# Eleven pairs of projections as block products in a stage of their own

## The chip, the cores and the metric

The kernel runs on one core of a Trainium2 chip. The metric is the device time of one execution in microseconds (us). Three runs of the kernel before took 1333.49, 1348.46 and 1333.42 us; their median is 1333.49 us.

## The reference

One encoder layer over 512 tokens of width 1024: a SwiGLU feed-forward layer, LayerNorm, a token mixer of three branches, LayerNorm, a second feed-forward layer, LayerNorm. All data are float32.

```python
proj = u @ w_in      # latents | dilated q, k, v | memory q | 3 gates
y_a = mla_attention(c_q, c_kv, k_rope, ...) @ w_br_mla       # 8 heads
y_b = dilated_attention(dil_cols) @ w_br_dil                 # 3 groups x 4 heads of 128
y_c = memory_attention(memq_cols, mem, w_mem_kv) @ w_br_mem  # 4 heads of 128
merged = sigmoid(g0) * y_a + sigmoid(g1) * y_b + sigmoid(g2) * y_c
h = layer_norm(ALPHA * h + merged @ w_o)
```

The change concerns the columns of `u @ w_in` that give dilated queries and keys (24 slices of 128 columns), memory queries (4 slices) and the gates (3 x 8 slices).

## The kernel before, in words

**Numbers.** Each float32 operand is kept as a high part `h` and a rest `l`. A weight tile is loaded from DRAM into one of three slots `raw` (SyncE, SP, issues it, L84), ScalarE (ACT) copies it to the high part (L87) and VectorE (DVE) subtracts that from it for the rest (L88). A product is three matmuls, high x high, high x rest, rest x high (`mm3`, L98 to L100). A result is split in the same way (L92, L93).

**Projections.** `proj` loads one 128-column slice of a weight (0.5 MB) and multiplies it with `u` in 8 steps of 128 rows: 24 matmuls that each stream 512 columns. `gate` puts a tanh behind it. `Gates.fill(n)` issues n of a gate's 8 steps, as work for TensorE (PE) between other steps. `y_a`, `y_b` and `y_c` multiply a branch's output with `w_br`: 12 matmuls of 512 columns each, two of them from one loaded weight.

**Quads.** The two feed-forward layers compute a pair of projections (gate and up) together: the pair is cut into blocks, and 7 block products of 12 matmuls with 256 columns, with sums of blocks on either side, give both results (`quad_load`, `quad_conv`, `quads`). I call one such pair a quad; it has 84 matmuls. Its sums of weights are formed by accumulating transfers that GpSimd (POOL) issues (L246, L247) onto parts that SP loaded (L243 to L245).

**Stages** (us of the span). Feed-forward layer 1 up to 345, with its quads from 33 to 229; memory keys and values, LayerNorm up to 402; latent attention up to 516; then `dil_v(0)`, six `y_a`, six projections `dil_proj` for head 0 and two `y_a` up to 604; four dilated heads up to 791; memory attention, with `y_b` and gates between its steps, up to 905; `y_c` and `w_o` up to 965; LayerNorm and layer 2 with its quads (1022 to 1205) to the end.

**A dilated head** is `dil_scores`, then cover work on PE, `dil_mix`, `dil_tr`, more cover work, `dil_pv`. Between scores and mix the row maxima and sums change their layout through DRAM: ACT stores them (L790, L791), POOL's queue loads them back (L792, L793), DVE combines them (L799 to L809) and scales the probabilities (L813). `dil_tr` transposes them (L825), ACT and DVE split them, and `dil_pv` uses them. In heads 0 to 2 the cover is four projections of the next head ahead of the mix and two behind the transposes; in head 3 it is gates.

**Order.** PE and SP run what is written in the order in which it is written (a manual schedule); the other engines' order is a scheduler's, except in the quads, where it is written too. Weight loads may be issued up to 200 priorities ahead, but SP's queue is in order: a load that waits for a free `raw` slot holds back all that are behind it.

Of the kernel before, what the change touches and what calls it, by code (L numbers as in the profile page):

```python
# [33 lines left out]
def build(tc, a, out):  # L34
# [141 lines left out]
    class FFN:  # L176
# [46 lines left out]
        def sums(self, xr):  # L223
# [10 lines left out]
            xh, xl = self.xT  # L234
            for i, j, c in ((1, 0, 0), (2, 1, 0), (4, 1, 1)):
                self.X[i] = tuple(x[:, 4 * j:4 * j + 4, c * 256:(c + 1) * 256] for x in self.xT)

        def quad_load(self, f):
            src = self.wgu[f]
# [40 lines left out]
        def quads(self, f0, f1, r):  # L280
            V = nc.vector
            m, u, sg = self.m, self.u, self.sg
            with tc.manual_schedule(engines={mybir.EngineType.DVE, mybir.EngineType.Activation, mybir.EngineType.Pool}):
# [5 lines left out]
                for f in range(f0, f1 + 1):  # L289
                    if f + 2 < f1:  # L290
                        r[f + 2] = self.quad_load(f + 2)
                    if f == f1 - 1:
                        self.s_r.close()
                        self.hc = pool("hc" + self.n, stack=self.stack, side="right")
# [11 lines left out]
                    if f == f1 - 1:  # L306
                        self.early = {c: self.h_pair(c, 0, S) for c in range(2)}
                    if prev is not None:
                        p, pa, pW = prev
                        self.prod(pa, pW, 4)  # L310
                        nc.scalar.activation(sg[:, 256:], pa, AF.Silu)
                        V.tensor_tensor(out=self.h(p), in0=u, in1=sg, op=OP.mult)
                    if f == f1:
                        break
                    self.prod(a, W, 6)
# [12 lines left out]
                    nc.scalar.activation(sg[:, :256], sg[:, :256], AF.Silu)  # L328
# [14 lines left out]
        def down(self, hf, toks, done, order=range(NF // 2), have={}, dest={}, mid=None):  # L343
# [17 lines left out]
            return kept  # L361

# [335 lines left out]
    mla_pv(7)  # L698
    s_a.close()


    s_b = ExitStack()
    bp = pool("dil", stack=s_b)
# [29 lines left out]
    def dil_proj(g, h, j):  # L733
        ps = proj(a["wdqk"][h, g, j], f"dp{g}{h}{j}")
        hl = bp.tile([P, 2, S], F32R, name=f"dhl{g}{h}{j}", tag="dqk", bufs=7)
        hi, lo = hl[:, 0], hl[:, 1]
        if g == 0:
            split(hi, lo, ps)
        else:
            split(hi.rearrange("p (r j) -> p r j", r=4), lo.rearrange("p (r j) -> p r j", r=4), ps.rearrange("p (j r) -> p r j", r=4))  # L740
        qkB[g, h, j] = (hi, lo, hl)

# [112 lines left out]
    def y_a(f):  # L855
        ps = branch_y(0, f, oA)
        nc.vector.scalar_tensor_tensor(out=acc[f], in0=acc[f], scalar=1.0, in1=ps, op0=OP.add, op1=OP.mult)
# [9 lines left out]
    s_oa.close()  # L867
# [16 lines left out]
    gb = Gates(1, [])  # L884
    for h in range(4):
        dil_scores(h)
        if h < 3:
            for g in range(2):
                for j in range(2):
                    dil_proj(g, h + 1, j)  # L890
        else:
            for f in range(4):
                sgB[f] = obp.tile([P, S], F32, name=f"sgB{f}", tag="sgB", bufs=4)
                gb.todo.append((1, f, sgB[f]))
            gb.fill(23)
        dil_mix(h)
        dil_tr(h)
        if h < 3:
            dil_proj(2, h + 1, 0)
            dil_proj(2, h + 1, 1)  # L900
        else:
            gb.fill(9)
        dil_pv(h)
        if h == 1:
            dil_v(1)
    s_q.close()
# [10 lines left out]
    qC, pC, tC, sgC = {}, {}, {}, {}  # L917

    def mem_q(h):
        ps = proj(a["wmq"][h], f"mq{h}")  # L920
        q = (cp.tile([P, S], F32R, name=f"mqh{h}", tag="mqh", bufs=2), cp.tile([P, S], F32R, name=f"mql{h}", tag="mql", bufs=2))
        split(q[0], q[1], ps)
        qC[h] = q
# [30 lines left out]
    def gate_c(f):  # L954
        sgC[f] = ocp.tile([P, S], F32, name=f"sgC{f}", tag="sgC", bufs=6)
        gate(2, f, sgC[f])
# [6 lines left out]

    mem_q(0)
# [3 lines left out]
    y_b(1)  # L968
    gate_b(4)
    mem_scores(0)  # L970
    y_b(2)
    gate_b(5)
    y_b(3)
    mem_tr(0)
    mem_q(1)
    mem_pv(0)
    gate_b(6)
    mem_scores(1)
    y_b(4)
# [76 lines left out]
    s_w.close()  # L1056
    s_acc.close()
# [54 lines left out]
def _pack(inputs):  # L1112
# [44 lines left out]
    A["wdqk"] = np.stack([np.stack([np.stack([fm(dil[:, j, g, h])[0] for j in range(2)]) for g in range(3)]) for h in range(4)])  # L1157
# [3 lines left out]
    A["wmq"] = fm(w_in[:, C_MQ:C_G])  # L1161
# [38 lines left out]
```

## Time and profile before

| | |
|---|---|
| median of three runs | 1333.49 us |
| profiled execution | 1332.55 us, span 1330.8 us |
| granted TensorE clock, mean | 0.997 |
| PE busy | 1310.9 us, 99% of the span |
| DVE, ACT, POOL busy | 65%, 46%, 8% |
| instructions of the span | 20,324 |

PE is the busy engine in every stage, so a stretch of the span is as long as PE's work in it, and time is lost where PE waits. The page gives busy shares, the chain that ended last, the costliest groups of instructions and the DMA issues; the stages are seen in a table of windows, single steps in the timeline of an engine.

### The profile page before, as it was taken

How to read it: one execution, taken by the hardware profiler on the slowest of the kernel's cores; microseconds unless marked ns; L12 is line 12 of the kernel's file. 1: busy time of each engine (PE TensorE's matmuls, PEld its weight loads, DVE VectorE, ACT ScalarE, POOL GpSimd, SP SyncE). 2: the span in 40 equal slices, each digit the busy share in tenths (PEclk: the TensorE clock that was granted, in tenths of full speed). 3: DMA queues.
4: the chain of work that ended last, by engine and by line, in shares of the span. 5: the costliest groups of instructions: out<-in, count | busy, mean ns of one | idle time of the engine just before them, and what ended most of it. 6: DMA issues, size and time to landing. Idle time of an engine off the chain costs nothing.

```text
span 1330.8 us, 20324 instructions
## 1 busy us (share of the span) xinstructions
PE 1310.9 (99%) x8036; PEld 1176.8 (88%) x8036; DVE 862.4 (65%) x1359; ACT 609.0 (46%) x987; POOL 109.0 (8%) x140
## 2 busy tenths in 40 slices
PE   8999999999999999999999999999999999999997
PEld 7999999888878879988899888888889999998885
DVE  8777776454748994435554556545798777774547
ACT  6555554433346773324334343343335555553332
POOL 1111110000101001000000000000011211100001
PEclk9999999999999999999999999999999999999998
DMA  8877775342544224322323323223666877764241
GB/s 259 211 185 203 190 199 176 118 143 95 163 154 143 58 64 79 127 95 88 72 80 103 96 65 127 80 80 95 215 220 188 207 183 199 193 184 131 99 155 64
DMA packets 70736, 185.75 MB, mean 140 GB/s; under 512 B 15728, under 2 KB 16368, under 8 KB 70640
## 3 DMA queue, kind: packets, MB, share of 16 engines
q1 hardware_dynamic: 49680, 159.73, 35.8%
q0 software_dynamic: 16736, 24.68, 11.4%
q8 instruction: 63, 1.03, 0.3%
q10 hardware_dynamic: 4224, 0.03, 0.2%
q14 instruction: 33, 0.27, 0.1%
HBM read 173.90 MB, written 7.37 MB: 136 GB/s over the span
## 4 chain that ended last, share of the span: by engine, by line
PE 91%; DVE 4%; DMA 2%; ACT 2%; issue 1%; POOL 0%; SPq 0%; POOLq 0%; DVEq 0%; ACTq 0%
PE dn L100 6%; PE dn L98 6%; PE dn L99 6%; PE ga L98 5%; PE ga L100 5%; PE ga L99 5%; PE dp L98 3%; PE dp L99 3%; PE dp L100 3%; PE g L98 3%; PE g L99 3%; PE gc L100 3%; PE gc L98 3%; PE g L100 3%; PE gc L99 3%; PE v L98 2%
## 5 line engine op out<-in xcount | busy, mean ns | idle before, releaser
L88 DVE TENSOR_TENSOR w<-raw,w 128x1024 fp32r<-128x1024 f32 x159 | 193.7, 1221 | 133.5 <-ACT w L87 129.0
L87 ACT ACTIVATE w<-raw 128x1024 fp32r<-128x1024 f32 x159 | 167.7, 1055 | 214.3 <-PE dp L99 45.9
L100 PE MATMUL dn<-w,hcl 128*128 128x512 f32 x320 | 124.6, 389 | 0.1
L99 PE MATMUL dn<-w,hch 128*128 128x512 f32 x320 | 124.5, 389 | 0.0
L98 PE MATMUL dn<-w,hch 128*128 128x512 f32 x320 | 124.5, 389 | 0.0
L263 DVE TENSOR_TENSOR w<-raw,w 128x1024 fp32r<-128x1024 f32 x78 | 95.1, 1219 | 1.9 <-ACT w L260 1.7
L260 ACT ACTIVATE w<-raw 128x1024 fp32r<-128x1024 f32 x78 | 82.0, 1052 | 8.8 <-DMA raw<-in_wgu 8.8
L98 PE MATMUL g<-uh,w 128*128 128x512 f32 x192 | 75.2, 391 | 0.0
L98 PE MATMUL dp<-uh,w 128*128 128x512 f32 x192 | 75.2, 391 | 0.0
L100 PE MATMUL g<-uh,w 128*128 128x512 f32 x192 | 74.8, 389 | 0.0
L100 PE MATMUL dp<-uh,w 128*128 128x512 f32 x192 | 74.8, 389 | 0.0
L99 PE MATMUL dp<-ul,w 128*128 128x512 f32 x192 | 74.7, 389 | 0.0
L99 PE MATMUL g<-ul,w 128*128 128x512 f32 x192 | 74.7, 389 | 0.0
L100 PEld LDWEIGHTS dn<-w,hcl 128*128 128x128 f32 x320 | 60.1, 188 | 13.1 <-DVE hcl L93 0.5
L99 PEld LDWEIGHTS dn<-w,hch 128*128 128x128 f32 x320 | 60.1, 188 | 12.5
L98 PEld LDWEIGHTS dn<-w,hch 128*128 128x128 f32 x320 | 60.1, 188 | 12.2
L93 DVE TENSOR_TENSOR hcl<-ha,hch 128x1024 fp32r<-128x1024 f32 (+2 forms) x35 | 35.1, 1009 | 53.3 <-ACT hch L92 53.3
L92 ACT ACTIVATE hch<-ha 128x1024 fp32r<-128x1024 f32 (+2 forms) x35 | 30.8, 887 | 74.9 <-PE dn L99 72.8
L263 DVE TENSOR_TENSOR w2l<-raw,w2h 128x1024 fp32r<-128x1024 f32 x39 | 47.8, 1225 | 20.6 <-ACT w2h L260 20.5
L328 ACT ACTIVATE sg<-sg 128x256 f32<-128x256 f32 x39 | 16.3, 419 | 86.2 <-DVE sg L327 86.2
L247 POOL DMA_DIRECT2D raw<-in_wgu x39 | 33.6, 862 | 248.8 <-DMA raw<-in_wgu 235.9
L93 DVE TENSOR_TENSOR hcl<-hb,hch 128x1024 fp32r<-128x1024 f32 (+2 forms) x20 | 20.2, 1011 | 49.7 <-ACT hch L92 49.7
(890 smaller groups left out, 4052.4 us busy)
## 6 DMA issues: line engine op xcount, KB each, us to landing
raw<-in_wgu SPq DMA_DIRECT2D x86, 512.0 KB, 5.8
raw<-in_wd SPq DMA_DIRECT2D x47, 512.0 KB, 3.4
raw<-in_wgu POOLq DMA_DIRECT2D x78, 256.0 KB, 5.7
raw<-in_wg SPq DMA_DIRECT2D x24, 512.0 KB, 3.6
raw<-in_wdqk SPq DMA_DIRECT2D x24, 512.0 KB, 3.3
raw<-in_wgu SPq DMA_DIRECT2D x42, 256.0 KB, 5.4
raw<-in_wo SPq DMA_DIRECT2D x16, 512.0 KB, 4.3
raw<-in_wv SPq DMA_DIRECT2D x12, 512.0 KB, 3.3
```

Of the source, the lines that this page charges most:

```text
L87: nc.scalar.activation(hi[:, c], raw[:, c], AF.Copy)
L88: (eng or nc.vector).tensor_tensor(out=lo[:, c], in0=raw[:, c], in1=hi[:, c].bitcast(F32), op=OP.subtract)
L92: nc.scalar.activation(hi, src, AF.Copy)
L93: nc.vector.tensor_tensor(out=lo, in0=src, in1=hi.bitcast(F32), op=OP.subtract)
L98: nc.tensor.matmul(ps, lh, rh, start=first, stop=False, **kw)
L99: nc.tensor.matmul(ps, lh, rl, start=False, stop=False, **kw)
L100: nc.tensor.matmul(ps, ll, rh, start=False, stop=last, **kw)
L247: nc.gpsimd.dma_start(r3[:, :S], src[:, 3 * S:], accum_op=OP.add)
L260: nc.scalar.activation(w[i][0], src, AF.Copy)
L263: nc.vector.tensor_tensor(out=w[i][1], in0=src, in1=w[i][0].bitcast(F32), op=OP.subtract)
L328: nc.scalar.activation(sg[:, :256], sg[:, :256], AF.Silu)
```

## The change

22 of the plain projections become 11 quads in a stage between the latent attention and the dilated heads: queries and keys of dilated groups 1 and 2 (16 slices, 8 pairs), memory queries 2 and 3, and the gates 0 to 3 of branch B. A class `Mix` reuses the quads with `u` as input. Its results are stored to DRAM by SP (`ahead`), the last ones by POOL (`rest`), and loaded again where they are used: `dil_back`, `mem_q`, `back_b`. All `y_a` now stand ahead of the quads, `dil_v(0)` behind them. In the heads, six gates of branch C take the place of the projections that went away. Memory queries 0 and 1 stay plain projections, ahead of the quads.

```diff
+    class Mix(FFN):
...
+        def fin(self, f, pa):
+            o = self.o[f]
+            if self.jobs[f][2]:
+                nc.scalar.activation(o[:, 0, 256:], pa, AF.Tanh, scale=0.5)
+                nc.scalar.activation(o[:, 1], o[:, 1], AF.Tanh, scale=0.5)
+            else:
+                nc.scalar.activation(o[:, 0, 256:], pa, AF.Copy)
+
+        def ahead(self, f):
+            if f - 2 in self.o:
+                nc.sync.dma_start(self.jobs[f - 2][1], self.o.pop(f - 2).rearrange("p a s -> p (a s)"))
...
+        def rest(self):
+            for f, o in self.o.items():
+                nc.gpsimd.dma_start(self.jobs[f][1], o.rearrange("p a s -> p (a s)"))
...
     mla_pv(7)
+    pmq = [proj(a["wmq"][h], f"mq{h}") for h in range(2)]
...
+    jobs = [(a["wdq"][h, g - 1], dp_d[g, h], False) for h in range(4) for g in (1, 2)]
+    jobs += [(a["wmq2"], mq_d[1], False)] + [(a["wgq"][i], gb_d[i], True) for i in range(2)]
+    mix = Mix(uT, jobs)
+    mix.open(s_p)
+    mix.sums()
...
+    for f in range(KT):
+        y_a(f)
+    mix.quads(0, len(jobs), {f: mix.quad_load(f) for f in range(2)})
+    mix.rest()
...
+    def dil_back(g, h):
+        with tc.high_priority(offset=AHEAD):
+            raw = rawp.tile([P, D], F32, name="raw", tag="raw", bufs=3)
+            nc.sync.dma_start(raw, dp_d[g, h])
+            for j in range(2):
+                hl = bp.tile([P, 2, S], F32R, name=f"dhl{g}{h}{j}", tag="dqk", bufs=6)
+                hi, lo = [hl[:, z].rearrange("p (r j) -> p r j", r=4) for z in range(2)]
+                split(hi, lo, raw[:, j * S:(j + 1) * S].rearrange("p (j r) -> p r j", r=4))
...
-    dil_v(0)
-    for f in range(6):
-        y_a(f)
-    for g in range(3):
-        for j in range(2):
-            dil_proj(g, 0, j)
-    y_a(6)
-    y_a(7)
...
+    for j in range(2):
+        dil_proj(0, 0, j)
+    dil_back(1, 0)
+    dil_back(2, 0)
+    dil_v(0)
     for h in range(4):
         dil_scores(h)
         if h < 3:
-            for g in range(2):
-                for j in range(2):
-                    dil_proj(g, h + 1, j)
+            for j in range(2):
+                dil_proj(0, h + 1, j)
+            gb.fill(5)
         else:
...
-            gb.fill(23)
+            gb.fill(20)
         dil_mix(h)
         dil_tr(h)
         if h < 3:
-            dil_proj(2, h + 1, 0)
-            dil_proj(2, h + 1, 1)
-        else:
-            gb.fill(9)
+            dil_back(1, h + 1)
+            dil_back(2, h + 1)
+        gb.fill(4)
         dil_pv(h)
...
     def mem_q(h):
-        ps = proj(a["wmq"][h], f"mq{h}")
...
+        qC[h] = wload(mq_d[h // 2][:, h % 2 * S:h % 2 * S + S], n=S, hp=q[0], lp=q[1])
...
+    back_b(0)
+    back_b(1)
     mem_q(0)
     wload(mk_d, hp=kC[0], lp=kC[1])
     wload(mv_d, hp=vC[0], lp=vC[1])
     y_b(0)
```

How the change moves instructions is shown at three places. First SP's queue, ahead of the heads. Before, from the last gates of the latent attention on (`in_wv1`, `in_wv0` are the weights of `dil_v(0)`, `in_wbr` those of `y_a`):

```order
L84 DMA raw_4981<-in_wg 128x1024
L84 DMA raw_5141<-in_wg 128x1024
L84 DMA raw_5196<-in_wv1 128x1024
L84 DMA raw_5200<-in_wv1 128x1024
L84 DMA raw_5204<-in_wv1 128x1024
L84 DMA raw_5208<-in_wv1 128x1024
L84 DMA raw_5322<-in_wv0 128x1024
L84 DMA raw_5326<-in_wv0 128x1024
L84 DMA raw_5434<-in_wbr 128x1024
```

Now, from the last store of the quads that SP issues (`om9` holds job 9's results, `dp_d` the stored queries and keys):

```order
L449 DMA gb_d0_5187<-om9_6516 128x1024
L84 DMA raw_6716<-in_wdqk 128x1024
L84 DMA raw_6748<-in_wdqk 128x1024
L878 DMA raw_6780<-dp_d10_5189 128x1024
L878 DMA raw_6788<-dp_d20_5190 128x1024
L84 DMA raw_6796<-in_wv1 128x1024
L84 DMA raw_6800<-in_wv1 128x1024
L84 DMA raw_6804<-in_wv1 128x1024
L84 DMA raw_6808<-in_wv1 128x1024
L84 DMA raw_6922<-in_wv0 128x1024
```

The four weight tiles of `dil_v(0)` stood behind gates; they now stand behind a store of the quads, two projection weights and two loads of stored results, all of which pass through the same three slots.

Second DVE, between the scaling of head 0's probabilities (`dp`) and the splits of their transposes (`t000h` and on); `dhl` are split queries and keys. Before:

```order
L813 TENSOR_SCALAR dp10_5768<-dp10_5768,z0_5975 128x256 x4
L88 TENSOR_TENSOR w_89<-raw_6051,w_89 128x1024
L93 TENSOR_TENSOR dhl011_5900<-dp011_5875,dhl011_5900 128x512
L88 TENSOR_TENSOR w_89<-raw_6198,w_89 128x1024
L93 TENSOR_TENSOR dhl110_5932<-dp110_5907,dhl110_5932 128x512
L88 TENSOR_TENSOR w_89<-raw_6230,w_89 128x1024
L93 TENSOR_TENSOR dhl111_5964<-dp111_5939,dhl111_5964 128x512
L93 TENSOR_TENSOR t000h_5992<-t000_5987,t000h_5992 128x512
L93 TENSOR_TENSOR t001h_6000<-t001_5995,t001h_6000 128x512
```

Now:

```order
L955 TENSOR_SCALAR dp10_7039<-dp10_7039,z0_7202 128x256 x4
L88 TENSOR_TENSOR w_89<-raw_7427,w_89 128x1024
L93 TENSOR_TENSOR dhl110_7248<-raw_7246,dhl110_7248 128x512
L93 TENSOR_TENSOR dhl111_7251<-raw_7246,dhl111_7251 128x512
L93 TENSOR_TENSOR dhl210_7256<-raw_7254,dhl210_7256 128x512
L93 TENSOR_TENSOR dhl211_7259<-raw_7254,dhl211_7259 128x512
L93 TENSOR_TENSOR dhl011_7171<-dp011_7146,dhl011_7171 128x512
L93 TENSOR_TENSOR t000h_7219<-t000_7214,t000h_7219 128x512
L93 TENSOR_TENSOR t001h_7227<-t001_7222,t001h_7227 128x512
```

Where three weight conversions and three splits of queries and keys stood ahead of the transposes' splits, there are now one conversion and five splits, four of them of stored results (`raw_7246`, `raw_7254`).

Third SP at the end of the heads. Before (`in_wmq` is the weight of the first memory query, `in_wbr` that of `y_b(0)`):

```order
L84 DMA raw_7300<-in_wg 128x1024
L84 DMA raw_7383<-in_wmq 128x1024
L84 DMA raw_7416<-mk_d_87 128x1024
L84 DMA raw_7420<-mv_d_88 128x1024
L84 DMA raw_7424<-in_wbr 128x1024
```

Now:

```order
L84 DMA raw_8239<-in_wg 128x1024
L68 DMA sgB0_8374<-gb_d0_5187 128x1024
L68 DMA sgB1_8376<-gb_d1_5188 128x1024
L84 DMA raw_8380<-mq_d0_5185 128x512
L84 DMA raw_8384<-mk_d_87 128x1024
L84 DMA raw_8388<-mv_d_88 128x1024
L84 DMA raw_8392<-in_wbr 128x1024
```

And DVE at the same place, now (`oBl` is the rest of head 3's output, `mql0` that of memory query 0; the last `w_89<-raw_8392` is `y_b(0)`'s weight):

```order
L994 TENSOR_TENSOR os3_8352<-do131_8335,os3_8352 128x2x128 x2
L93 TENSOR_TENSOR oBl_6706<-os3_8352,oBh_6705 128x512
L88 TENSOR_TENSOR mql0_8379<-raw_8380,mqh0_8378 128x512
L88 TENSOR_TENSOR kCl_8371<-raw_8384,kCh_8370 128x1024
L88 TENSOR_TENSOR vCl_8373<-raw_8388,vCh_8372 128x1024
L88 TENSOR_TENSOR w_89<-raw_8392,w_89 128x1024
```

The weight of `y_b(0)` is now loaded behind two gates' results, a memory query and the memory keys and values; the slot that it takes is freed by `mql0`, which on DVE stands behind `oBl`. The projection of memory query 0, which stood ahead of `y_b(0)` on PE, is gone from there.

## Rows read from the trace of the kernel before

**Rows 1.** Page part 1: busy us, share of the span, instructions of each engine.

```profile
PE 1310.9 (99%) x8036; PEld 1176.8 (88%) x8036; DVE 862.4 (65%) x1359; ACT 609.0 (46%) x987; POOL 109.0 (8%) x140
```

**Rows 2.** Windows of two stages; the header names the columns.

```profile
core 0: us, PE busy (x) PEld busy (x) DVE busy (x) ACT busy (x) POOL busy (x), PEclk, DMA share, GB/s
...
33.00:229.00 196.00, 196.00 (x1700) 194.81 (x1700) 146.21 (x201) 109.64 (x183) 30.23 (x35) 1.00 0.74 196
...
604.00:791.00 187.00, 187.00 (x1008) 165.92 (x1008) 99.03 (x256) 72.63 (x146) 8.36 (x17) 1.00 0.30 84
```

**Rows 3.** Waits of PE past the first matmuls: us in total, times, longest us.

```profile
PE c L99 <- DVE w L88: 0.8, 1, 0.8
```

**Rows 4.** Timeline of PE: a dilated projection's start, the end of six.

```profile
565.97 0.39 PE L98 MATMUL dp<-uh,w 128*128 128x512 f32 x1
...
598.61 0.39 PE L98 MATMUL y<-oAh,w 128*128 128x512 f32 x1
```

**Rows 5.** Timeline of PE: one product's start in two neighbouring quads.

```profile
37.02 0.28 PE L98 MATMUL gd<-xh,w 128*128 128x256 f32 x1
...
46.54 0.28 PE L98 MATMUL gd<-xh,w 128*128 128x256 f32 x1
```

**Rows 6.** Timeline of DVE: last split of the latent attention's output.

```profile
517.76 0.69 DVE L93 TENSOR_TENSOR oAl<-oas,oAh 64x512 fp32r<-64x512 f32 x1 [0.70 <-ACT oAh L92]
```

**Rows 7.** Page part 5: conversions of a loaded weight (busy, mean ns).

```profile
L88 DVE TENSOR_TENSOR w<-raw,w 128x1024 fp32r<-128x1024 f32 x159 | 193.7, 1221 | 133.5 <-ACT w L87 129.0
L87 ACT ACTIVATE w<-raw 128x1024 fp32r<-128x1024 f32 x159 | 167.7, 1055 | 214.3 <-PE dp L99 45.9
```

**Rows 8.** DMA issues: count, KB each, median us to landing.

```profile
raw<-in_wgu SPq DMA_DIRECT2D x86, 512.0 KB, 5.8
...
raw<-in_wgu POOLq DMA_DIRECT2D x78, 256.0 KB, 5.7
...
raw<-in_wv SPq DMA_DIRECT2D x12, 512.0 KB, 3.3
```

**Rows 9.** Timeline of PE, heads 0 and 3: scores end; transposes begin and end.

```profile
607.22 0.45 PE L98 MATMUL dp<-uh,w 128*128 128x512 f32 x1
...
764.30 0.45 PE L98 MATMUL g<-uh,w 128*128 128x512 f32 x1
...
780.03 0.27 PE L825 MATMUL t<-ident,dp 128*128 128x128 f32 x1
...
781.70 0.48 PE L98 MATMUL g<-uh,w 128*128 128x512 f32 x1
```

**Rows 10.** Timeline of DVE, the same heads: mixing weights, scaling, last transposed split.

```profile
621.02 0.17 DVE L799 TENSOR_TENSOR mm<-dst 128x8 f32<-128x8 f32 x1 [5.37 <-DMA dst<-x]
...
622.60 2.12 DVE L813 TENSOR_SCALAR dp<-dp,z 128x192 f32<-128x192 f32 x8
...
776.98 0.17 DVE L799 TENSOR_TENSOR mm<-dst 128x8 f32<-128x8 f32 x1 [4.42 <-DMA dst<-x]
...
783.55 0.67 DVE L93 TENSOR_TENSOR t131h<-t,t131h 128x512 fp32r<-128x512 f32 x1
```

**Rows 11.** Timeline of PE: the first memory query, behind head 3.

```profile
791.15 0.46 PE L98 MATMUL mq<-uh,w 128*128 128x512 f32 x1
```

**Rows 12.** Timeline of DVE: the last split of head 3's output.

```profile
797.27 0.69 DVE L93 TENSOR_TENSOR oBl<-os,oBh 128x512 fp32r<-128x512 f32 x1 [0.76 <-ACT oBh L92]
```

**Rows 13.** Windows: around TensorE's last matmul.

```profile
1320.00:1325.00 5.00, 0.97 (x5) 0.47 (x3) 4.93 (x9) 0.00 (x0) 1.93 (x2) 0.85 0.42 174
1325.00:1331.00 6.00, 0.00 (x0) 0.00 (x0) 1.98 (x3) 0.00 (x0) 0.98 (x1) 0.50 0.30 117
```

**Rows 14.** Timeline of PE: three of the first matmuls of the program.

```profile
9.00 0.41 PE L98 MATMUL gv<-xh,w 128*128 128x256 f32 x1
9.21 0.41 PE L99 MATMUL gv<-xl,w 128*128 128x256 f32 x1
...
12.62 0.36 PE L100 MATMUL gu<-xh,w 128*128 128x256 f32 x1
```

More of the change, by code (lines that the diff above doesn't have):

```diff
@@ L233, in sums, with direct, src, sgu @@
             split(*self.X[7], t[7])
-            xh, xl = self.xT
+            self.direct()
+        def direct(self):
             for i, j, c in ((1, 0, 0), (2, 1, 0), (4, 1, 1)):
                 self.X[i] = tuple(x[:, 4 * j:4 * j + 4, c * 256:(c + 1) * 256] for x in self.xT)
+        def src(self, f):
+            return self.wgu[f]
+        def sgu(self, f):
+            return self.sg, self.u
+        def c11(self, f, x):
+            nc.scalar.activation(x, x, AF.Silu)
+        def fin(self, f, pa):
+            nc.scalar.activation(self.sg[:, 256:], pa, AF.Silu)
+            nc.vector.tensor_tensor(out=self.h(f), in0=self.u, in1=self.sg, op=OP.mult)
+        def ahead(self, f):
+            pass
+        def late(self):
+            self.s_r.close()
+            self.hc = pool("hc" + self.n, stack=self.stack, side="right")
+        def split_early(self):
+            self.early = {c: self.h_pair(c, 0, S) for c in range(2)}
         def quad_load(self, f):
-            src = self.wgu[f]
+            src = self.src(f)
             r1 = self.rq.tile([P, D], F32, name="raw1", tag="raw1", bufs=2)
@@ L289, in quads @@
                 for f in range(f0, f1 + 1):
+                    self.ahead(f)
                     if f + 2 < f1:
@@ L292, in quads @@
                     if f == f1 - 1:
-                        self.s_r.close()
-                        self.hc = pool("hc" + self.n, stack=self.stack, side="right")
+                        self.late()
                     g = self.quad_conv(f + 1, r[f + 1]) if f + 1 < f1 else None
@@ L306, in quads @@
                     if f == f1 - 1:
-                        self.early = {c: self.h_pair(c, 0, S) for c in range(2)}
+                        self.split_early()
                     if prev is not None:
@@ L698, in build, with y_a, gate_tile @@
     mla_pv(7)
+    mq_d = [dram.tile([P, D], F32, name=f"mq_d{i}") for i in range(2)]
+    gb_d = [dram.tile([P, D], F32, name=f"gb_d{i}") for i in range(2)]
+    dp_d = {(g, h): dram.tile([P, D], F32, name=f"dp_d{g}{h}") for h in range(4) for g in (1, 2)}
+    pmq = [proj(a["wmq"][h], f"mq{h}") for h in range(2)]
     s_a.close()
-    s_b = ExitStack()
+    s_p = ExitStack()
+    jobs = [(a["wdq"][h, g - 1], dp_d[g, h], False) for h in range(4) for g in (1, 2)]
[3 more added lines that the diff above has]
+    mix.sums()
+    om = mix.out("mq")
+    for j in range(2):
+        nc.scalar.activation(om[:, j], pmq[j], AF.Copy)
+    nc.gpsimd.dma_start(mq_d[0], mix.o.pop("mq").rearrange("p a s -> p (a s)"))
+    def y_a(f):
+        ps = branch_y(0, f, oA)
+        nc.vector.scalar_tensor_tensor(out=acc[f], in0=acc[f], scalar=1.0, in1=ps, op0=OP.add, op1=OP.mult)
+    for f in range(KT):
+        y_a(f)
+    wat[0] = 24
+    mix.quads(0, len(jobs), {f: mix.quad_load(f) for f in range(2)})
+    wat[0] = 0
+    mix.rest()
+    s_p.close()
+    s_oa.close()
+    s_b = ExitStack()
+    s_g = ExitStack()
+    gcp = pool("sgc", stack=s_g, side="right")
+    sgC = {}
+    def gate_tile(f):
+        sgC[f] = (gcp if f < 6 else ocp).tile([P, S], F32, name=f"sgC{f}", tag="sgC", bufs=6 if f < 6 else 2)
+        return sgC[f]
     bp = pool("dil", stack=s_b)
@@ L954, in gate_c @@
     def gate_c(f):
-        sgC[f] = ocp.tile([P, S], F32, name=f"sgC{f}", tag="sgC", bufs=6)
-        gate(2, f, sgC[f])
+        gate(2, f, gate_tile(f))
     def y_c(f):
@@ L1056, in build @@
     s_w.close()
+    s_g.close()
     s_acc.close()
```

139 lines of the change are left out of this document (92 added, 47 removed).

## The prediction

> **What bounds the kernel now.** I read the busy times first: PE works in 99% of the span, 1310.9 of 1330.8 us [rows 1], so what the change gives is what it takes from PE's work, and what it costs is time in which PE waits. The windows by stage say the same of the two stages that matter here, the feed-forward quads and the dilated heads: PE is busy throughout, at granted clock 1.00, with the DMA engines 0.74 busy in the quads and 0.30 in the heads [rows 2]. The waits of PE show how little is left to win by covering better: past the first matmuls the longest is 0.8 us [rows 3]. The timelines then give the price of each kind of work on PE, and the chains of other engines that today's cover hides.
>
> **What the change takes off PE.** Six projections run from 565.97 to 598.61 [rows 4]: 32.64 / 6 = 5.44 us each, 0.227 us for each of 24 matmuls. A quad takes 46.54 - 37.02 = 9.52 us [rows 5], 0.113 us for each of 84 matmuls of half the columns. 22 projections cost 119.7 us, 11 quads 104.7 us: **15.0 us less**, if every quad finds its weights and nothing else waits. Everything else on PE only moves.
>
> **What it adds, place by place, in us of PE waiting.**
>
> *Start of the quads.* PE has two memory queries and eight `y_a` left (2 x 5.44 + 8 x 2.72 = 32.6), from about 516 to 548.5. DVE is free for the block sums when the last attention output is split, 518.45 [rows 6]: eight sums and differences and four splits of 1024 columns at 1.22 [rows 7], 14.6, with up to six weight conversions between, 7.3: done at 533 to 540. They sit in the quads' own load buffers, so the first weights' chain comes behind: load 5.8, accumulating load 5.7 [rows 8], conversion 1.06 [rows 7]. Ready at 546 to 553: 0 to 4.5, taken 0.5, since the conversions are spread over the time in which sums wait for nothing.
>
> *Within the quads.* A quad moves 196 GB/s x 9.52 us = 1.87 MB at a DMA share of 0.74 [rows 2]. Each now also stores 0.52 MB: share 0.74 x 2.39 / 1.87 = 0.95. That is under 1, so no wait is forced; but SP issues the store of job f-2 ahead of the loads for f+2, and waits there for the result. Bounds: 0, and 10 quads late by half of what a store takes at this rate (0.52 MB / 265 GB/s = 2.0), 10. Taken 2.
>
> *End of the quads.* The weight of the next projection stands in SP's queue behind the store of job 9, which waits for the tanh of a result that PE finishes only some 6 us before its last quad ends; load 3.3 [rows 8], conversions 1.06 and 1.22 [rows 7]. PE, with nothing else to do, waits about 2.7 (2 to 3.5).
>
> *`dil_v(0)`.* Its cover was eight MLA heads long; now its four tiles come through three slots, two of which hold stored results that wait to be split. Three tiles pass one slot in turn, 3.3 + 1.06 + 1.22 = 5.6 each, so the third has its high part 2 x 5.6 + 4.4 = 15.6 after the slot came free; PE has about 9.3 of the two projections and 2 x 1.36 of the first tiles, 12.0, and needs the rest too, 1.2 later. 3.6 to 4.8; taken 5 with the fourth tile, bounds 0 to 9.
>
> *Heads, scores to transposes.* In head 0 the mixing weights are started at 621.02, 13.8 us after the last score at 607.22, in head 3 at 776.98, 12.7 after 764.30 [rows 9, 10]; what they waited for is the round trip of small transfers through DRAM. The scaling starts 1.58 later and half of its 2.12 must be done [rows 10]: 2.6. PE's cover was 21.8 (four projections); it becomes two projections and five gate steps, 10.9 + 3.4 = 14.3, in head 3 20 steps, 13.6. So PE waits 13.8 + 2.6 - 14.3 = 2.1 in each of three heads and 1.7 in head 3. In head 3 five more loads (gates' results, memory query, keys and values, 2.4 MB) are issued just when the small transfers run. 8.0 by the rows, taken 10; 4 if each round trip comes a microsecond earlier, 14 if the loads hold them up.
>
> *Heads, transposes to `dil_pv`.* From the first transpose to the last split takes 780.03 to 784.22, 4.2; PE has 1.67 of transposes [rows 9, 10] and now 12 matmuls, 2.7, together 4.4. That just covers, but in head 0 five splits (0.67 each) now stand on DVE ahead of the transposes' own. 0 to 3.2 in three heads; taken 3 in all, bounds 0 to 7, `dil_v(1)`'s slots with it.
>
> *Start of the memory stage.* This is the largest. PE comes to `y_b(0)` directly behind head 3's products, where a memory query of 5.44 used to stand [rows 11]. `y_b(0)`'s weight can be loaded only when the slot of memory query 0 is free, whose conversion stands on DVE behind `oBl`. `oBl` ended 6.8 after those products [rows 11, 12]; without the weight conversions ahead of it on ACT and DVE some 3.5 to 4.5. Then the query's rest 0.6, load 3.3 [rows 8], high part 1.06, rest 1.22 [rows 7], less 0.45 that PE can do with the high part: 9.2 to 10.2. Taken 9.3, bounds 7 to 12. The rest of the memory stage has the same work in another order, with shorter covers: 1 (0 to 4).
>
> *Clock.* With PE at work no window stands below 1.00, but around its last matmul it is 0.85 and then 0.50 [rows 2, 13]; and the program's first matmuls, behind an idle start, come 0.21 us apart, twice 0.113, the rate of 1.2 GHz instead of 2.4. 17 steps from 9.00 to 12.62 [rows 14] lose 0.1 each, 1.7 us. I take one such loss, for the 9.3 us wait; bounds 0 and 5.1 (also `dil_v(0)` and head 3). The Trainium skill, "TensorE: Matmul & The Clock Gate", section "HAM oscillation", says that a kernel whose waits for DMA are long enough returns to the slow clock behind every one of them. By that rule the three longest waits would each pay, 3.4 more and 1357 in all; if the clock held through all of them it would be 1352.
>
> **Sum.** Waits 0.5 + 2 + 2.7 + 5 + 10 + 3 + 9.3 + 1 + 1.7 = 35.2; less 15.0: **+20.2 us**. The profiled execution took 1332.55, 0.94 under the median of the runs, so 1352.8 against it, and **1354** as a median: 1.5% slower, which a limit of 2% (1360.2, 1306.8), about what a measurement of this kernel tells from no change, calls the same.
>
> **Rivals.**
>
> *The covers hold.* The chains in the quads, `dil_v(0)` and the heads are made of transfers. In the heads the DMA engines are 0.30 busy [rows 2], and a head's weight loads fall from six to two and two loads of results. If the round trips in the heads come in within 11.7 us instead of 13.8 and the slots free in time, the 2 + 5 + 10 + 3 go; 15.2 are left against 15.0, and the time is 1334, not slower. It decides at 11.7 us from last score to mixing weights. For it: 99% busy today. Against it: 12.7 is the shortest that I see, with the fewest loads beside it. 0.17, with 1325 to 1340.
>
> *The stores collide with the quads' loads.* At a DMA share of 0.95, with SP waiting for results in front of loads, each quad may run late. If the quad's period grows from 9.52 to above 10.4, 8.5 us more than none and 6.5 more than I count, the kernel is over 1360; late by 1.5 each it is 15 - 2 = 13 above my sum, 1367. The same place on the time line is reached when head 3, `dil_v(0)` and the memory start all pay the clock. For it: today the quads' loads take 5.8 where a 0.5 MB load elsewhere takes 3.3 [rows 8]. Against it: two quads of prefetch. 0.32, with 1360 to 1385.
>
> *The change does not do what it says.* If the 11 groups did not replace the 22 projections, PE's work would not fall, and with the waits the time would be 1369. PE's list of instructions has 84 matmuls for each pair and none of the 22, so 0.01.
>
> My forecast has 0.50, with 1340 to 1360. Faster by 2% would need 26.7 us off, more than the 15.0 that exist: 0.01. Within 2%: 0.50 + 0.16. Slower: 0.32 + 0.01. The range leaves out the lower half of the first rival and the end of the second: 1332 to 1374.
>
> **What would show it.** In the profile after: quads 9.52 us apart, and DMA near 0.95 in their windows; PE waits on a weight at `dil_v(0)` and at `y_b(0)`, the latter some 9 us and the longest; waits of 1 to 5 us ahead of the transposes of each head, on the scaling; granted clock below 1.00 right behind the longest wait, and matmuls 0.21 or 0.45 us apart there. I am wrong if PE's waits past the first matmuls add up to less than 15 us, or if most of them lie within the quads.

## The result: 3% slower

The changed kernel takes 1379.38 us (median of 4 runs, 1377.24 to 1380.53), the kernel before 1337.92 in the runs beside it: a ratio of 1.0296, 95% interval 1.0226 to 1.0367. The prediction, 1354 in a range up to 1374, was too low; it stays so if the 4.4 us are taken off by which the kernel before was slower beside it than in the runs (1333.49) that the prediction starts from. The profiled execution took 1377.24, its span 1375.2: 44.4 us more than the span before, where +20.2 was forecast.

### The profile page after: what moved, and what is told of

Same layout as the page of the kernel before. It is cut to its first block, busy times and chain, and to the rows that moved or that the text cites. A ratio compares the mean times of both kernels' runs of the same rounds, so it can differ in the third digit from the quotient of the medians.

```text
span 1375.2 us, 21471 instructions
## 1 busy us (share of the span) xinstructions
PE 1319.4 (96%) x8432; PEld 1193.3 (87%) x8432; DVE 928.4 (68%) x1448; ACT 653.7 (48%) x1059; POOL 130.2 (9%) x164
## 4 chain that ended last, share of the span: by engine, by line
PE 77%; DVE 9%; DMA 8%; ACT 3%; issue 2%; POOL 0%; SPq 0%; POOLq 0%; DVEq 0%; ACTq 0%
PE ga L98 6%; PE ga L99 6%; PE ga L100 6%; PE dn L100 5%; PE dn L99 5%; PE dn L98 5%; PE gc L98 3%; PE gc L99 3%; PE gc L100 3%; DMA raw<-in_wgu 2%; DMA x<-dst 2%; PE g L98 2%; PE g L99 2%; PE g L100 2%; PE gd L99 2%
## 5 line engine op out<-in xcount | busy, mean ns | idle before, releaser
L98 PE MATMUL g<-uh,w 128*128 128x512 f32 x160 | 64.2, 401 | 0.0
L99 PE MATMUL g<-ul,w 128*128 128x512 f32 x160 | 63.0, 394 | 0.0
L100 PE MATMUL g<-uh,w 128*128 128x512 f32 x160 | 62.8, 393 | 0.0
L247 ACT ACTIVATE sg<-sg 128x256 f32<-128x256 f32 x39 | 16.3, 419 | 86.2 <-DVE sg L352 86.2
L93 DVE TENSOR_TENSOR hcl<-hb,hch 128x1024 fp32r<-128x1024 f32 (+2 forms) x20 | 20.2, 1011 | 49.4 <-ACT hch L92 49.4
L98 PE MATMUL ga<-x7h,w 128*128 128x256 f32 x156 | 43.6, 279 | 3.5 <-ACT m L341 3.5
L92 ACT ACTIVATE hch<-hb 128x1024 fp32r<-128x1024 f32 (+2 forms) x20 | 17.8, 890 | 60.2 <-PE dn L99 60.2
L98 PE MATMUL v<-w,uh 128*128 128x512 f32 (+1 forms) x112 | 40.5, 362 | 4.2 <-ACT w L87 4.2
```

Source lines behind the costliest of these rows:

```text
L92: nc.scalar.activation(hi, src, AF.Copy)
L93: nc.vector.tensor_tensor(out=lo, in0=src, in1=hi.bitcast(F32), op=OP.subtract)
L98: nc.tensor.matmul(ps, lh, rh, start=first, stop=False, **kw)
L99: nc.tensor.matmul(ps, lh, rl, start=False, stop=False, **kw)
L100: nc.tensor.matmul(ps, ll, rh, start=False, stop=last, **kw)
L247: nc.scalar.activation(x, x, AF.Silu)
```

## The profile after

Page part 1, busy us, share of the span and instructions of each engine, against [rows 1]:

```profile
PE 1319.4 (96%) x8432; PEld 1193.3 (87%) x8432; DVE 928.4 (68%) x1448; ACT 653.7 (48%) x1059; POOL 130.2 (9%) x164
```

PE has less to compute and yet is busy for 8.5 us more: some of its matmuls became slower. Its idle time grew from 20 to 56 us. The waits of PE (us in total, times, longest us), of which the longest before was 0.8 [rows 3]:

```profile
PE t L967 <- DVE dp L955: 9.0, 4, 3.7
PE y L98 <- ACT w L87: 7.9, 1, 7.9
...
PE v L98 <- ACT w L87: 4.2, 2, 2.4
PE ga L98 <- ACT m L341: 3.5, 1, 3.5
...
PE do L99 <- DVE t020h L93: 1.5, 1, 1.5
```

From the top: transposes (`t`) that wait for scaled probabilities in all four heads; `y_b(0)` on its weight; `dil_v(0)` on its weights (`v`); one late quad of the second feed-forward layer (`ga`, 3.5); a head's first products (`do`) on split transposes. Windows of the new stage, of that part of it in which loads still run, of the two projections with `dil_v(0)`, of the heads, and around `y_b(0)`, against [rows 2]:

```profile
core 0: us, PE busy (x) PEld busy (x) DVE busy (x) ACT busy (x) POOL busy (x), PEclk, DMA share, GB/s
549.00:661.00 112.00, 108.97 (x924) 108.14 (x923) 74.21 (x101) 54.02 (x89) 15.60 (x18) 1.00 0.77 210
565.00:634.00 69.00, 69.00 (x592) 69.00 (x591) 47.09 (x64) 34.43 (x56) 11.72 (x14) 1.00 0.92 247
661.00:702.00 41.00, 33.62 (x124) 28.09 (x125) 14.20 (x15) 14.02 (x17) 4.94 (x8) 0.88 0.58 153
702.00:873.00 171.00, 157.65 (x884) 140.00 (x884) 97.21 (x252) 74.86 (x144) 9.03 (x17) 0.98 0.30 90
...
877.00:881.00 4.00, 0.00 (x0) 0.00 (x0) 2.36 (x2) 1.90 (x3) 0.00 (x0) 0.50 0.64 206
881.00:885.00 4.00, 3.76 (x8) 2.56 (x9) 2.00 (x3) 1.83 (x3) 0.00 (x0) 0.50 0.74 225
885.00:889.00 4.00, 4.00 (x14) 3.15 (x14) 2.92 (x4) 1.06 (x1) 0.00 (x0) 0.75 0.63 224
```

The column before the DMA share is the granted clock. It fell while PE waited for `y_b(0)`'s weight, to 0.50 (1.2 GHz), and stayed there for 12 matmuls; the last two windows hold 8 and 14 matmuls, where 4 us at full clock hold 18 (the window of e9_warmy below). It fell at four more places, behind waits in `dil_v(0)` (2.44), ahead of the transposes of heads 0 and 1 (2.75 and 3.66) and in the second feed-forward layer (3.50):

```profile
678.00:688.00 10.00, 6.91 (x13) 4.01 (x13) 6.62 (x6) 5.36 (x6) 0.00 (x0) 0.54 0.57 200
741.00:744.00 3.00, 3.00 (x12) 2.52 (x11) 3.00 (x4) 3.00 (x6) 0.00 (x0) 0.56 0.44 137
774.00:778.00 4.00, 4.00 (x17) 3.30 (x15) 4.00 (x7) 4.00 (x7) 0.54 (x2) 0.57 0.00 0
1078.00:1081.00 3.00, 3.00 (x16) 3.00 (x16) 3.00 (x7) 0.64 (x3) 0.00 (x0) 0.52 0.59 96
```

Timelines of PE: `y_b(0)`, head 0's end of scores (the projection behind them) and transposes, one product's start in two neighbouring quads of the new stage, and in two of the second feed-forward layer:

```profile
873.03 0.22 PE L988 MATMUL do<-t131h,v1l 128*128 128x128 f32 x1
881.20 0.79 PE L98 MATMUL y<-oBh,w 128*128 128x512 f32 x1 [7.94 <-ACT w L87]
...
883.48 0.63 PE L99 MATMUL y<-oBl,w 128*128 128x512 f32 x1
883.90 0.63 PE L100 MATMUL y<-oBh,w 128*128 128x512 f32 x1
...
721.43 0.45 PE L98 MATMUL dp<-uh,w 128*128 128x512 f32 x1
...
738.73 3.13 PE L967 MATMUL t<-ident,dp 128*128 128x128 f32 x16 [2.75 <-DVE dp L955]
741.51 0.77 PE L98 MATMUL g<-uh,w 128*128 128x512 f32 x1
...
600.31 0.28 PE L98 MATMUL ga<-uh,w 128*128 128x256 f32 x1
610.14 0.28 PE L98 MATMUL ga<-uh,w 128*128 128x256 f32 x1
...
1072.76 0.28 PE L98 MATMUL gd<-h2h,w 128*128 128x256 f32 x1
1077.79 0.39 PE L98 MATMUL ga<-x7h,w 128*128 128x256 f32 x1 [3.50 <-ACT m L341]
1087.67 0.28 PE L98 MATMUL gd<-h2h,w 128*128 128x256 f32 x1
```

Matmuls that last 0.63 and start 0.42 to 0.43 apart are at half rate; at full rate they last 0.39 and start 0.23 apart. The new stage's quads are 9.80 to 9.83 apart where [rows 5] has 9.52, and no wait stands between them.

DVE in head 0, against [rows 10]:

```profile
736.77 0.17 DVE L941 TENSOR_TENSOR mm<-dst 128x8 f32<-128x8 f32 x1 [4.02 <-DMA dst<-x]
...
738.35 2.12 DVE L955 TENSOR_SCALAR dp<-dp,z 128x192 f32<-128x192 f32 x8
740.39 1.22 DVE L88 TENSOR_TENSOR w<-raw,w 128x1024 fp32r<-128x1024 f32 x1
741.53 4.08 DVE L93 TENSOR_TENSOR dhl<-raw,dhl 128x512 fp32r<-128x512 f32 x4
...
746.13 0.67 DVE L93 TENSOR_TENSOR t000h<-t,t000h 128x512 fp32r<-128x512 f32 x1
```

From the last score (721.43) to the mixing weights (736.77) it is 15.3 us here, 13.8 before; in the four heads 13.0 to 16.2, where it was 12.7 to 16.3. So the round trip through DRAM takes about as long as before; what PE had to do meanwhile is shorter. Behind the scaling, four splits of stored queries and keys stand ahead of the first transposed split. They take 1.02 each, that one 0.67: they read every fourth element of a tile in on-chip memory.

Stage by stage, what the span lost against the ideal (PE's work of before, less 15.0). "Waits" is time in which PE had nothing to do, "half rate" what matmuls took longer at a granted clock of 0.50; what is left of "lost" are steps that were slower for other reasons:

| stage (us of the span) | predicted | lost | of it waits | half rate |
|---|---|---|---|---|
| quads and their start (515 to 662) | 5.2 | 9.8 | 5.8 | 0 |
| two projections, `dil_v(0)` (to 718) | 5 | 10.9 | 7.4 | 3.1 |
| heads (to 873) | 13 | 22.2 | 13.5 | 2.4 |
| memory stage (to 953) | 10.3 + clock 1.7 | 11.1 | 8.1 | 2.6 |
| second feed-forward layer, tail | 0 | 6.0 | 3.5 | 1.7 |
| sum | 35.2 | 60.0 | 38.3 | 9.8 |

## The experiments

Theory 1: the loss is made of single waits, each where the change took PE's cover away, and each wait brings a stretch at half rate; the work saved is real. Theory 2: the stage itself is dear (its traffic, its queues), or the waits pass on to the next step as soon as one is removed. All ratios are against the kernel before, with 95% intervals. In the runs beside the experiments its median moved between 1335.0 and 1340.8, so a total says little about a few us; these are read from stretches of the profiles.

**e1_mem.** `y_b(0)`'s weight is loaded ahead of the last products, and a gate of branch B stands before `y_b(0)`.

```diff
+    hoist(1)      # wload of y_b's first weight, behind head 3
...
+    gate_b(4)
     y_b(0)
...
-    gate_b(4)
```

> Changed against the kernel of the change: the first weight of y_b is loaded ahead of the gates' results, memory query and keys, and gate B4 stands ahead of y_b(0) on PE instead of behind memory scores. Nothing is left out. Theory 1 (the loss is PE's waits where covers are gone, and the slow clock behind each): the 8.1 us wait ahead of y_b(0) falls under 1 us, the 12 slow matmuls behind it go too (2.5 us), so 9 to 11 us less than the 1377 to 1380 of the change. Theory 2 (the loss is added DRAM traffic, and a wait that is removed comes back at the next load): the wait moves to the next weight or to memory scores, and less than 4 us are won.

1383.41 us, 1.0339 (1.0293 to 1.0385), not below the change. `y_b(0)` no longer waits, but from the last head product to `y_c` it took 78.9 us against 80.4: 1.5 won of 8. The waits in the memory stage, then ACT there:

```profile
PE ms L99 <- DVE kCl L88: 3.1, 1, 3.1
...
PE y L98 <- ACT w L87: 2.3, 1, 2.3
```

```profile
882.89 0.60 ACT L565 ACTIVATE sgB<-g 128x512 f32<-128x512 f32 x1 [3.23 <-PE g L100]
883.38 0.62 ACT L87 ACTIVATE mqh<-raw 128x512 fp32r<-128x512 f32 x1
```

ACT put the moved gate's tanh ahead of the conversions of the memory query and of the keys and values behind it; it waits 3.23 for PE, and the slots for the next loads come free behind it. The wait moved to the memory scores (`ms`) and to the next weight of the `y_b` (`y`): theory 2 in this place, a miss for theory 1.

**e2_dilv.** `dil_v(0)` ahead of the two projections.

```diff
+    dil_v(0)
     for j in range(2):
         dil_proj(0, 0, j)
     dil_back(1, 0)
     dil_back(2, 0)
-    dil_v(0)
```

> Changed against the kernel of the change: dil_v(0) stands ahead of the two projections and the two loads of stored results instead of behind them. Nothing is left out. Theory 1 (dil_v(0) lost 11 us since its four weight tiles came through the slots behind stored results): its tiles now take three slots at once, its waits of 7.4 us fall to 2 to 4 including the one at the end of the quads, no slow clock there: 5 to 8 us less. Theory 2 (traffic: the gather of u's edges, a store and the loads share the DMA engines at this point): the wait is as long, only on other instructions: within 2 us of the change.

1375.83, 1.0297 (1.0256 to 1.0338). The stage took 48.7 for 55.9, as theory 1 has it, and its clock stayed full; but PE now waited longer for `y_b(0)`, and the heads took some 3 us more. A window of the stage, and that wait:

```profile
661.00:710.00 49.00, 46.85 (x243) 43.43 (x242) 17.39 (x18) 16.39 (x22) 4.93 (x8) 1.00 0.56 153
```

```profile
PE y L98 <- ACT w L87: 12.4, 1, 12.4
```

**e3_act.** ACT's queue stores the results of the quads, not SP's.

```diff
-                nc.sync.dma_start(self.jobs[f - 2][1], ...)
+                nc.scalar.dma_start(self.jobs[f - 2][1], ...)
```

> Changed against the kernel of the change: the stores of the quads' results are issued by ACT, which makes the results, instead of SP. Nothing is left out. Theory 1 (SP's queue waits at the stores): the 2.4 us wait at the end of the quads goes, since the next weights are loaded while the last quad runs; the quads' period stays 9.82 us; 2 to 3 us less. Theory 2 (the stores in SP's queue also make the quads slow): the period falls to 9.52 us, 5 to 6 us less.

1374.06, 1.0309 (1.0248 to 1.0369). The stage with `dil_v(0)` 50.5 for 55.9, the quads' stage 112.0 for 113.6, their period the same 9.82. DMA issues from 655 to 712 (count, KB each, median us to landing); in the change the first took 3.9 and the store 3.0:

```profile
raw<-in_wv SPq DMA_DIRECT2D x6, 512.0 KB, 3.3
...
gb_d<-om ACTq DMA_DIRECT2D x1, 512.0 KB, 2.6
```

So SP's waits for results did hold back the loads at the end of the stage, and cost nothing within it.

**e4_off** and **e8_u8.** Where the operands of the quads lie in on-chip memory. In the feed-forward layers the input starts 8 elements and the weights 24 into their tiles; in the new stage `u` starts at 0, its sums at 8, the weights at 24. e4 puts all at 0; e8 puts `u` at 8 and, outside the stage too, all weights at 24, so that within the stage only `u` moves.

```diff
e4 +        wo = 0       # in Mix; weights, and X[i] = x[:, :D]
e8 -    uT = xpair("u")
e8 +    uT = xpair("u", 8)
e8 -    wat[0] = 0       # twice: weights stay at 24 in the stages that use u
```

> Changed against the kernel of the change: within the new quads the operands' tiles start at offset 0, as u does, instead of at 8 (block sums) and 24 (weights) elements. Nothing is left out. The new quads came 9.82 us apart, those of the feed-forward layers 9.52, with every matmul 3% slower and no wait. Theory 1 (the place of the operands in SBUF): the period falls to 9.5 to 9.6, 2 to 3 us less. Theory 2 (the added traffic slows PE's reads): the period stays at 9.8 and the time within 1 us.

> Changed against the kernel of the change: u starts 8 elements into its tile, and all weight tiles 24, as in the feed-forward layers, for all stages that use u. Nothing is left out. Theory 1 (the new quads are 3% slower because of where operands lie against one another in SBUF): they come 9.5 to 9.6 us apart; plain projections may get slower. Theory 2 (it is the traffic of the stores or other engines' work): 9.8 us as in the change.

e4 1383.99, 1.0358 (1.0319 to 1.0396); e8 1390.97 in its one run. One product's start in neighbouring quads of the stage, of e4 and then of e8:

```profile
609.94 0.28 PE L98 MATMUL ga<-uh,w 128*128 128x256 f32 x1
620.02 0.28 PE L98 MATMUL ga<-uh,w 128*128 128x256 f32 x1
```

```profile
572.27 0.28 PE L98 MATMUL ga<-uh,w 128*128 128x256 f32 x1
581.79 0.28 PE L98 MATMUL ga<-uh,w 128*128 128x256 f32 x1
```

10.08, 9.82 and 9.52: the period goes with the place of the operands, and not with the stores, which are the same in all three. e4's expected sign was wrong, e8 showed the matter. The change's period, 9.78 and 9.86 in turn, stands in all eleven profiles that have its offsets, wherever no quad is late; 10.08 and 9.52 are from one execution each. e8's time is high for other reasons: the quads of its second feed-forward layer ran 9.89 apart behind a late one, two quads of the new stage were late by 1.7 and 1.1, its heads took 3.8 us more, and `y_c` took 22.5 for 21.8.

**e5_warm** and **e9_warmy.** Idle matmuls of 512 columns fill PE's waits, to see whether the clock then stays up: e5 ahead of `y_b(0)` and of the transposes of heads 0, 1 and 3, e9 ahead of `y_b(0)` alone.

```diff
+    def idle(n):
+        ps = bank("idle")
+        for i in range(n):
+            nc.tensor.matmul(ps, uT[0][:, 0, :P], uT[0][:, 1], start=i == 0, stop=i == n - 1)
...
+    idle(34)
     y_b(0)
```

> Added to the kernel of the change: matmuls of 512 columns whose results nobody reads, in the places where PE waits anyway: 34 (7.7 us) ahead of y_b(0), 8, 12 and 8 (1.8, 2.7, 1.8 us) ahead of the transposes of heads 0, 1 and 3. No wait's end is changed. Theory 1 (the granted clock falls in the waits, and what follows runs at half rate): the 12 slow matmuls behind y_b(0) and those behind the transposes go, granted clock 1.00 there; 3 to 5 us less than the change. Theory 2 (the slow steps come from other traffic at these places, not from the clock): as many slow steps as before, and the time is the same or up to 2 us more.

> Added to the kernel of the change, at one place alone: 34 matmuls of 512 columns (7.7 us) whose results nobody reads, ahead of y_b(0), where PE waits 8.1 us. Theory 1 (clock): no slow matmuls behind y_b(0), the stretch from the first y_b to the first y_c 2 to 2.6 us shorter (70 us instead of 72.3), the rest as in the change. Theory 2 (other traffic): 72.3 as before.

e5 1390.07, 1.0367 (1.0303 to 1.0431); e9 1377.44, 1.0294 (1.0214 to 1.0374). Behind e9's `y_b(0)`, started at 888.64:

```profile
890.00:894.00 4.00, 4.00 (x18) 3.34 (x19) 2.27 (x3) 1.27 (x2) 0.00 (x0) 1.00 0.58 204
```

From `y_b(0)` to `y_c` e9 took 70.1 for 72.3 and e5 70.2: the clock's price behind this one wait is 2.1 to 2.2 us. In the heads the idle matmuls were themselves in the way (167.6 for 154.8), and the clock fell there all the same, behind waits that were left: a miss. The total shows nothing of e9's gain: its quads' stage took 119.1 for 113.6 in the profile, with late quads, one 14.64 behind the one before it.

**e6_pipe.** The products of head h stand behind the scores of head h+1, as cover for its round trip.

```diff
         dil_scores(h)
+        if h > 0:
+            dil_pv(h - 1)
...
+        gb.fill((8, 4, 0, 20)[h])
```

> Changed against the kernel of the change: within the heads, the products of head h stand behind the scores of head h+1, dil_v(1) with them, and the gate steps are spread anew (8, 4, 0, 20 between scores and transposes, 2 behind), so that PE has 16.3 to 16.9 us, in head 2 over 40, between a head's scores and its transposes, instead of 14.3 and 13.6. Nothing is left out. Theory 1 (the heads lose 22 to 27 us since PE's cover is shorter than the round trip through DRAM): the waits ahead of the transposes fall from 9.7 us to under 3, the heads get 10 to 18 us shorter. Theory 2 (the round trip grows with what PE does, since weight loads for the cover hold up the small transfers): the waits stay above 7 us and less than 4 us are won.

1375.62, 1.027 (1.0216 to 1.0325). Heads 150.2 for 154.8. The waits:

```profile
PE t L967 <- DVE dp L955: 4.3, 3, 2.0
...
PE ds L922 <- DVE dhl L93: 2.9, 3, 1.6
PE ds L99 <- DVE dhl L93: 2.2, 1, 2.2
```

The transposes' waits are halved, and the scores (`ds`) now wait for the splits of stored queries and keys. 4.6 us were won, where theory 1 had 10 to 18 and theory 2 less than 4: neither by its numbers. The chain from the last score to the mixing weights grew as well, as theory 2 has it: 16.7, 17.7 and 15.6 us in heads 0, 1 and 3, for 15.3, 16.2 and 14.1 in the change.

**e7_all** and **e10_all2.** The edits together: e2, e3 and e6, block sums in the other of the two load buffers, `y_b(0)`'s weight ahead with gate steps alone in front; in e7 the stored queries and keys are split late in a head, in e10 loaded and split right behind the scores.

```diff
+        gb.fill(2)
+        dil_split(1, h + 1)      # e7
+        dil_split(2, h + 1)
...
         dil_scores(h)
+        dil_back(1, h + 1)       # e10
+        dil_back(2, h + 1)
```

> All edits that attack a wait together: results stored by ACT; dil_v(0) ahead of the projections; heads as in the run before; splits of stored queries and keys behind those of the transposes; the first weight of y_b loaded ahead of the memory loads and the last gate steps ahead of y_b(0); block sums held in the other load buffer, so that the first quad's first load can start earlier. Nothing is left out. Theory 1 (the waits are 44 us, and go where cover is given back): 25 to 40 us less than the change, 1340 to 1355; with all of the 15 us of saved work it would come to 1325. Theory 2 (waits move on): over 1365.

> As the run with all edits together, but the stored queries and keys of the next head are loaded and split right behind a head's scores, ahead of its mixing weights, instead of behind its transposes. Nothing is left out. Theory 1 (in the run with all edits the heads still waited 12 us for splits that were late and the clock that fell there): the waits ahead of scores and products fall under 4 us, the heads from 151 us to 138 to 145, and the time from 1358 to 1343 to 1352. Theory 2 (these splits only move the wait to the mixing weights): 1355 to 1362.

e7 1357.92, 1.0161 (1.0095 to 1.0227), 21.5 below the change; e10 1359.81, 1.0137 (1.0075 to 1.0199). In e7 the two projections and `dil_v(0)` took 45.9, 1.0 more than the ideal, and `y_b(0)` did not wait; the heads still took 151.0. e7's total lies between the two theories, e10's in the range of its theory 2. What waits in e7 and then in e10:

```profile
PE ds L937 <- DVE dhl L93: 5.4, 4, 2.0
...
PE g L98 <- ACT w L87: 2.7, 1, 2.7
```

```profile
PE t L975 <- DVE dp L963: 6.2, 2, 3.3
```

Splitting late makes the scores wait, splitting early the scaling and so the transposes. As long as the heads have this little PE work of their own, the order of that work moves the wait and does not end it.

**e11_part.** The eight dilated pairs are plain projections in the heads again; the stage keeps the three pairs of memory queries and gates.

```diff
-    jobs = [(a["wdq"][h, g - 1], dp_d[g, h], False) for h in range(4) for g in (1, 2)]
-    jobs += [(a["wmq2"], mq_d[1], False)] + ...
+    jobs = [(a["wmq2"], mq_d[1], False)] + ...
...
+            for g in range(2):
+                for j in range(2):
+                    dil_proj(g, h + 1, j)
-            gb.fill(5)
```

> The change, but the 8 pairs of dilated queries and keys (groups 1 and 2) are computed plainly between the heads' steps again, as before the change; only the memory queries and the gates B0 to B3 stay in the stage of block products. Theory 1 (the change loses because the work that lay between the heads' steps, ahead of the transposes and beside dil_v(0), was taken away): the 8 plain pairs cost 8 x (10.88 - 9.82) = 8.5 us more on TensorE than in block products, but the heads have no wait of more than 1 us ahead of a transpose and take near 187 us as before the change, and what was lost at dil_v(0) (8 to 11) and in the heads (22) comes back: 1350 to 1357 in all. Theory 2 (the loss is in the stage itself and its traffic through DRAM, whatever covers the heads): 1372 or more.

1355.97 (10 runs), 1.0112 (1.0078 to 1.0147): 23.4 below the change, although PE has 8.5 us more to do. The heads in a window, and the longest wait of its profile:

```profile
652.00:841.00 189.00, 187.77 (x1011) 166.34 (x1009) 96.10 (x255) 70.70 (x145) 8.37 (x17) 1.00 0.24 66
```

```profile
PE y L98 <- ACT w L87: 11.8, 1, 11.8
```

Heads 188.5 (before 187.0), no wait ahead of a transpose, clock 1.00; the stage with `dil_v(0)` lost 2.9 where the change lost 10.9. Theory 1 by its numbers: the heads lost what their cover had hidden. A rival is that e11 also takes the loads and splits of stored results out of the heads. It does not explain the transposes: from the last score to the mixing weights it is still 12.3 to 16.2 us, and only PE's work beside it has grown. For the products (`do`, 3 us in all), whose splits stood behind those of stored results, the two are not told apart. `y_b(0)`'s wait stays, even longer.

**e12_part2.** e11 with the stores on ACT's queue, the block sums in the other buffer, and `y_b(0)`'s weight ahead with five gate steps in front. The edit also changes the order of the steps behind `y_b(1)` in the memory stage, which the expectation does not name.

```diff
-                nc.sync.dma_start(self.jobs[f - 2][1], ...)
+                nc.scalar.dma_start(self.jobs[f - 2][1], ...)
...
+    hoist(1)
+    gb.fill(48)
```

> The kernel of e11_part, and the stage's results are stored by ScalarE's queue, its block sums lie in the other of two buffers, and the memory stage's first weight is loaded ahead with the gate's steps in front of y_b(0). Theory 1 (what is left to lose after e11 is the start of the memory stage, some 8 us, and the start of the quads, some 4): 1335 to 1345, no longer slower than before the change by over 1%. Theory 2 (the waits only move to the next step): above 1350.

1346.74 (10 runs), 1.0040 (1.0003 to 1.0076): 32.6 below the change, 1.7 above theory 1's range, and less than its 1% slower than the kernel before. How much of the 9.2 us against e11 each of its edits gave is not shown. The longest wait in heads and memory stage, then two neighbouring quads of its second feed-forward layer:

```profile
PE g L98 <- ACT w L87: 3.0, 1, 3.0
```

```profile
1051.66 0.28 PE L98 MATMUL gd<-h2h,w 128*128 128x256 f32 x1
1061.55 0.28 PE L98 MATMUL gd<-h2h,w 128*128 128x256 f32 x1
```

Of the 13.5 us by which its span (1344.3) is above the span before, 6.7 are those quads, 9.89 and not 9.52 apart all through a layer that the edit does not touch. No version beats the kernel before.

## Why the prediction was wrong

**The gain was right.** 11 quads for 22 projections, 15.0, less 3.1: the quads ran at 9.82 instead of 9.52, which e8 puts down to where `u` lies.

**The step that failed is the term for the clock.** I took one loss of 1.7 for all the waits. Five stretches at half rate cost 9.8: 3.1 at `dil_v(0)`, 2.4 in heads 0 and 1, 2.6 at `y_b(0)`, 1.7 in the second feed-forward layer (of the other profiles only those of e3 and e8 show a fall there). I had taken the clock to fall behind the longest wait alone; in this trace it fell behind each of the five waits of 2.44 us and more (past the first matmuls), and not behind head 3's of 2.18. The one loss was sized too small besides: at `y_b(0)` it was 2.1 to 2.2 by e5 and e9, and the row that I read 1.7 from begins at 9.00, while the slow matmuls had begun with the first one, at 4.51.

The Trainium skill, "TensorE: Matmul & The Clock Gate", section "HAM oscillation", says that a kernel with long enough waits for DMA goes back to the slow clock behind every one of them. The trace agrees with it, at 0.50 in the windows at `y_b(0)`, and goes beyond the three waits that I let it price, at 1357.

The clock is the largest of several terms, not the whole miss. It makes 8.1 of the 24.8 us by which the loss (60.0) is above my sum (35.2); with it right I would have said 1362.

**Right in place and size:** transposes 9.7 (10 predicted), products with the short waits beside them 3.8 (3), `y_b(0)` 8.1 (9.3), end of the quads 2.4 (2.7). The longest single wait is the one that I named. For the transposes the sum is partly luck: the single waits were 2.75, 3.66, 0.45 and 2.18, not 2.1 and 1.7, since the chain to the mixing weights varied from 13.0 to 16.2 us; and the transposes began 0.38 behind the scaling's start, not when half of it was done.

**Right in place, too small:** the start of the quads 4.3 for 0.5, near its upper bound (with the block sums in the other buffer, in e7, e10 and e12, the first quad's last product began 2.9 to 3.9 us earlier, counted from the first memory query: the sums do delay the first weights). The stage with `dil_v(0)` 7.4 for 5: the store and the loads in SP's queue held it up (e2, e3), and POOL's loads of the edges of `u` and its last store ran beside the first of its weight tiles (7.0 and 6.8 us to landing); what these added is not shown by a run.

**Not in the sum:** 6.3 us more in the heads, about half of it transposes that follow the scaling one by one (2.3 to 2.8 us a head for 1.66 before) and steps of a few tenths; and 5.2 in the second feed-forward layer, whose second quad waited 3.5 behind an accumulating load that took 8.1 us to land. Its period there was 9.67 before, 14.91 in the change and 9.7 to 14.1 in the profiles of e1 to e7 and e9, so part of it is scatter.

**The traffic in the quads was right, its price was not.** I had a DMA share of 0.95 there. While loads still run it is 0.92, at 247 GB/s x 9.82 us = 2.43 MB for a quad, near the 2.39 of the prediction; the 0.77 of the whole stage takes in the last two quads, beside which no weight of a quad is loaded. Yet no quad was late, where I took 2. The rival of colliding stores names the right time, 1360 to 1385, for a wrong reason: e3 took the stores off SP and the period stayed, and e8 with the same stores has 9.52. Only what it says of several places that pay the clock came true, and head 3 was not one of them. The first rival, that the covers hold, fell: it needed 11.7 us from the last score to the mixing weights, and in head 0 it is 15.3.

What stays open: why a layer's quads run at 9.52 in some executions and at 9.89 in others (e4 and e5 in the first layer and e8 and e10 in the second, behind a late second quad; e11 and e12 in the second from its start). It is worth 6 to 7 us, and the scatter of the kernel before, 1334 to 1350, may be of this kind; its one profile shows 9.52. So a period of one execution does not rest on the place of the operands alone.

## What to carry to other kernels

Work that PE does between two steps of a chain is not only work, it is the cover of that chain: before moving it away to do it cheaper, count for each place how long the chain is and what PE has left, and add what the clock costs behind each wait (here it fell behind waits of 2.44 us and more). The saving was 1.36 us a pair, and a pair in the heads was 10.9 us of cover for a round trip through DRAM of 12.7 to 16.3 us. Taking away one wait moved it to the next step four times here (e1, e2, e6, e10); giving the heads their work back (e11) ended the waits there.

## What the runs showed of the hardware that was not expected

- The same 84 matmuls took 9.52, 9.82 or 10.08 us with their operands at three places in on-chip memory (e8, the change, e4), with no wait between them in the trace. The first and the last are from one execution each.
- The granted clock was 0.56 from 741 to 744, behind a wait of 2.75 us, and 1.00 again from 744 on.
- The split of 128x512 elements took 1.07 us on DVE and 1.16 on ACT where it reads every fourth element of a tile in on-chip memory (the change), 0.68 and 0.58 from PE's accumulator (the kernel before), and 0.69 on DVE from a tile in on-chip memory without the step [rows 12].
